# Two edits in the second feed-forward layer: an earlier place for four seven-product units, and another order of the row tiles in every down-projection

## The chip, the cores and the metric

The kernel runs as one launch on one core of a Trainium2 chip. The metric is the device time of that launch in microseconds (us); lower is better. Times of the kernel before are the median of three runs.

## What is computed

Two layers of an encoder trunk on 256 tokens of width 2048, in float32. The first layer mixes tokens by pooling and grouped-query attention, the second by a bidirectional matrix-memory recurrence. Each mixer is followed by the same feed-forward block, and only that block is touched here. Cut to what matters:

```python
D_MODEL, SEQ, D_FF = 2048, 256, 5632

def conv_ffn(x, w_up, conv_w, conv_b, w_down):
    u = x @ w_up                                   # 256 x 11264: a gate half and a value half
    up = jnp.pad(u, ((0, 0), (1, 1), (0, 0)))
    u = c[0] * up[:, :-2] + c[1] * up[:, 1:-1] + c[2] * up[:, 2:] + conv_b
    gate, val = jnp.split(u, 2, axis=-1)
    return (jax.nn.silu(gate) * val) @ w_down

for layer in range(2):
    h = rms_norm(x, norm_mix[layer])
    x = x + mixer(h)                               # attention + pooling, then the recurrence
    x = x + conv_ffn(rms_norm(x, norm_ffn[layer]), w_up[layer], conv_w[layer], conv_b[layer], w_down[layer])
```

## The kernel before

**Number format.** Every float32 operand of a matmul is split into a high and a low part (`hl`, `xx`, `g` hold both). A product is three matmuls: high by high, high by low, low by high. Weights come from memory in entries of 128 x 1024 floats (512 KB). For each entry SyncE (SP) issues the load into a tile `w`, ScalarE (ACT) rounds it to the high part (line 152), and VectorE (DVE) subtracts to get the low part (line 153). The class `Stream` does this in the order of one list for the whole program; in a feed-forward layer it loads up to eight entries ahead of the one TensorE (PE) uses and splits up to four ahead.

**The hidden layer in chunks.** The 5632 hidden columns are 44 row tiles of 128, in six chunks of 4, 8, 8, 8, 8 and 8 (`FCH`). The tiles of a chunk are kept in one buffer `g` (`gt` in the code), rows 0 to 7; two such buffers alternate between the chunks. A chunk is made by the up-projection and then read by the down-projection of that chunk, in four column blocks of 512 (`down`, one accumulation in PSUM for each block).

**Two ways to make row tiles.** A plain row tile (`up`) takes four weight entries of 16 matmuls each, and is followed by a tail: ScalarE copies the sum, VectorE adds and scales it (lines 446 and 990), then the convolution (lines 971, 972, 974), the gate (977, 978) and the split into high and low (979 on ScalarE, 980 on VectorE). Four row tiles together can instead be made by a *unit* (`quads`), which computes a 2 x 2 block product with seven block products in place of eight. A unit takes 28 entries with 6 matmuls each: eight that are accumulated in two PSUM banks, eight in two further banks, and twelve that add to them. The weight sums that it needs are made beforehand in device memory by accumulating transfers issued from GpSimd (POOL); the steps of that work (`_make_steps`) are tied to fixed positions in the list of entries. For eight of the last twelve entries of a unit VectorE adds two halves of the entry first (line 140).

When a unit's last product is done, two tasks are queued: `finish` of its third and fourth row tile 3 us later, and `finish` of its first and second row tile 11 us later (lines 1085 and 1086). Each task makes one row tile, waits 4 us, and makes the other: four transposes on PE (line 1096), a copy on ScalarE (line 1098), then the tail. These delays are in a virtual time that is advanced as matmuls are issued. PE runs strictly in the written order; on ScalarE, VectorE and SP a planner orders the instructions by times that it works out itself.

For the second half of a chunk (rows 4 to 7), the rows thus get ready in the order 6, 7, 4, 5.

**Order of the work.** `_ffn_plan(layer)` writes the order of PE's work in a feed-forward layer. It lists slots: one slot is one entry of a plain row tile (`n`, 16 matmuls) or one entry of a down-projection (`d`, two row tiles, 12 matmuls). `UNITS[layer]` then gives for each unit its chunk, its half, a first and a last slot, and how its sums are made; the 28 entries of the unit (`s`) are spread between these two slots. The second layer has six units: the first half of chunk 3, and the second half of chunks 1, 2, 3, 4 and 5. From slot 72 on, its slots are: 72 to 87 the down-projection of chunk 2; 88 to 103 the plain rows of chunk 4; 104 to 119 the down-projection of chunk 3; 120 to 135 the plain rows of chunk 5; 136 to 151 the down-projection of chunk 4; then the down-projection of chunk 5, whose last column block is written apart (`down_end`).

```python
    for c, h, lo, hi, kind in UNITS[layer]:
        one, two = 2 * m, m + m // 2                    # m = 8: 16 and 12 entries
        long = 1.25 if kind == 3 else 1.0
        step = (hi - lo - 3) / (one * long + two)
        for k in range(one + two):
            at = k * long if k < one else one * long + k - one
            here[int(lo + at * step + (3 if k >= one else 0))].append(("s", c, h))
```

Two things guard the units. The second half of a unit's first sixteen entries waits until both `finish` tasks of the unit before it have been issued (`late`, line 1046). And the transposes of `finish` use the same two PSUM banks that this second half uses.

In `down`, `kts` is the order in which the row tiles of `gt` are read, two for each weight entry; `_ffn_order` puts the entries of the weights in the same order.

Of the kernel before, what the change touches and what calls it, by code (L numbers as in the profile page):

```python
# [30 lines left out]
DFF = 5632  # L31
FT = DFF // P
FCH = [4, 8, 8, 8, 8, 8]
CH = 8
NEG = -1.0e30
NGATE = 96 + 8
# [28 lines left out]
class Stream:  # L65
# [16 lines left out]
    def load(self, pieces=1):  # L82
        i = self.n_load
        src = self.srcs[i]
        kind, src = src if isinstance(src, tuple) else ("plain", src)
        w = self.home(i, True).tile([P, CH * P], F32, tag="w", name=f"w{i}")
        if kind in ("made", "have"):
            width = n = CH * P
            at = 0
# [56 lines left out]
    def split(self, then=None):  # L146
        i = self.n_split
        self.sums(i)
        w, n, width = self.w.pop(i)[:3]
        hl = self.home(i, False).tile([P, 2, CH * P], F32R, tag="hl", name=f"hl{i}")  # L150
        for c in range(0, width, n):
# [82 lines left out]
def trunk(ctx: ExitStack, tc: tile.TileContext, gx, xT, xn, call, catt, cml, weights, make, out):  # L234
# [169 lines left out]
    def mov_part(ps, act, kts, first, last):  # L404

        n = len(kts)
        hl = None
        for i, k in enumerate(kts):
            if i % 2 == 0:
                hl = st.next()  # L410
            src, c = act(k), i % 2 * 512
            wh, wl = hl[:, 0, c : c + 512], hl[:, 1, c : c + 512]
            for t in range(2):
                xh, xl = (src[:, j, t * P : t * P + P] for j in range(2))
                mm(ps[:, t], xh, wh, first and i == 0, False)
                mm(ps[:, t], xh, wl, False, False)
                mm(ps[:, t], xl, wh, False, last and i == n - 1)
            wv.tick(1.29)

    def mov_group(act, name, width=512, before=None, after=None):  # L420

        ps = mmp.tile([P, 2, 512 if width > 256 else width], F32, tag="mm", name=name)
        per = CH * P // width
        hl = None
# [27 lines left out]
    def residual(ps, b, eng=None):  # L452
        for t in range(2):
            xs = x[:, t, b * 512 : b * 512 + 512]
            v.tensor_add(xs, xs, ps[:, t])
# [495 lines left out]
    def ffn_layer(layer, norm, nxt):  # L951
        with ExitStack() as es:
# [29 lines left out]
            def up(f, gt, i):  # L982
                ps = mmp.tile([P, 2, 2, S], F32, tag="mm", name=f"up{layer}_{f}")
                for q in range(KT // 4):
                    stat_part(ps, xx, list(range(4 * q, 4 * q + 4)), q == 0, q == KT // 4 - 1)
                    if q < KT // 4 - 1:
                        yield
                wv.until(lambda: norm.R is not None)
                u = gather(tp, ps, f"up{layer}_{f}")
                v.tensor_mul(u, u, bc(norm.R, 2))  # L990
                tail(u, f, gt, i)
# [111 lines left out]
            def down_end(gt, b, kts):  # L1103

                parts = [(0, 0, 512), (1, 0, 512)]
                pss = [psp.tile([P, 512], F32, tag="ps", name=f"end{i}") for i in range(2)]
                n = len(kts)

                def terms(i, k, hl):
                    t, c0, c1 = parts[i]  # L1110
                    ps = pss[i][:, : c1 - c0]
                    wh, wl = (hl[:, j, k % 2 * 512 + c0 : k % 2 * 512 + c1] for j in range(2))
                    xh, xl = (gt[:, k, j, t * P : t * P + P] for j in range(2))
                    mm(ps, xh, wh, k == kts[0], False)
                    mm(ps, xh, wl, False, False)
                    mm(ps, xl, wh, False, k == kts[-1])

                for k in kts[:-2]:
                    if k % 2 == 0:
                        hl = st.next()  # L1120
                    for i in range(2):
                        terms(i, k, hl)
                hl = st.next()
                for i, (t, c0, c1) in enumerate(parts):
                    for k in kts[-2:]:
                        terms(i, k, hl)
                    xs = x[:, t, b * 512 + c0 : b * 512 + c1]
                    v.tensor_add(xs, xs, pss[i][:, : c1 - c0])
                    nc.sync.dma_start(out[:, t, b * 512 + c0 : b * 512 + c1], xs)

            def down(c, gt, b):
                kts = list(range(FCH[c]))
                last = c == len(FCH) - 1
                if last and nxt is None and b == NB - 1:
                    down_end(gt, b, kts)
                    return
                ps = mmp.tile([P, 2, 512], F32, tag="mm", name=f"dn{layer}_{c}_{b}")
                for k in range(0, len(kts), 2):
                    mov_part(ps, lambda k: gt[:, k], kts[k : k + 2], k == 0, k == len(kts) - 2)
                    if k < len(kts) - 2:  # L1140
                        yield
                residual(ps, b)
                if last and nxt is None:
                    nc.sync.dma_start(out[:, :, b * 512 : b * 512 + 512], x[:, :, b * 512 : b * 512 + 512])
                elif last:
                    nxt.add(b)
                yield
# [15 lines left out]
            def g_of(c):  # L1163
                if c not in gts:
                    gts[c] = actp.tile([P, 8, 2, S], F32R, tag=f"B{c % 2}", name=f"g{layer}_{c}")
                return gts[c]

            for step in _ffn_plan(layer):
                kind, c = step[:2]
                key = step[:3]  # L1170
                if key not in run:
                    f0 = sum(FCH[:c])
                    run[key] = (up(f0 + step[2], g_of(c), step[2]) if kind == "n" else
                                down(c, gts[c], step[2]) if kind == "d" else
                                quads([f0 + 4 * step[2] + j for j in range(4)], c, 4 * step[2], f"{layer}_{c}{step[2]}",
                                      (c, step[2]) in apart))
                next(run[key], None)
# [15 lines left out]
def _stat(w, kts):  # L1193

    k = len(kts)
    t = w.reshape(k, P, 2, P)[:, :, :, :]
    return t.reshape(k // 4, 4, P, 2, P).transpose(0, 2, 1, 3, 4).reshape(k // 4, P, CH * P)


def _mov(w):  # L1200

    return w.reshape(-1, 2, P, 512).transpose(0, 2, 1, 3).reshape(-1, P, CH * P)

# [38 lines left out]
def _down_chunks(w):  # L1242
    out, k0 = [], 0
    for n in FCH:
        rows = w[k0 * P : (k0 + n) * P]
# [4 lines left out]

UNITS = (
    ((1, 1, 17, 38, 2), (2, 1, 45, 64, 2), (3, 1, 71, 100, 3), (4, 1, 107, 129, 2), (5, 1, 136, 158, 2)),
    ((1, 1, 17, 37, 2), (2, 1, 38.5, 59, 2), (3, 0, 60.5, 80, 2), (3, 1, 81.5, 99, 2), (4, 1, 100.5, 123, 2),
     (5, 1, 124.5, 146, 2)),
)


def _ffn_plan(layer):

    slots = []  # L1260
    for c, n in enumerate(FCH):
        fill = [("n", c, i) for i in range(n) if not any(u[0] == c and u[1] == i // 4 for u in UNITS[layer])]
# [7 lines left out]
        for e in fill:  # L1270
            slots += [e] * (4 if e[0] == "n" else FCH[e[1]] // 2)
    here = [[] for _ in slots]
# [29 lines left out]
def _ffn_order(layer, up, dn, four, last):  # L1302

    pos, seq = {}, []
    m = KT // 2
    d0 = [sum(FCH[:c]) // 2 * NB for c in range(len(FCH))]
    for step in _ffn_plan(layer):
        kind, c, i = step
        n = pos.get(step, 0)
        pos[step] = n + 1  # L1310
        if kind == "n":
            seq.append(up[(sum(FCH[:c]) + i) * 4 + n])
        elif kind == "d":
            seq.append(dn[d0[c] + i * (FCH[c] // 2) + n])
        else:
            u = [e[:2] for e in UNITS[layer]].index((c, i))
            made = UNITS[layer][u][4]
            if n >= 2 * m and (n - 2 * m) % 3 == 2:
                seq.append(last[u, (n - 2 * m) // 3])
                continue  # L1320
            second = n >= m if made in (1, 2) else n % 2
            at = (n - 2 * m) // 3 * 2 + (n - 2 * m) % 3 if n >= 2 * m else n % m if made in (1, 2) else n // 2
            q, key = four[u, at], f"{layer}{c}{i}_{at}"
            if n >= 2 * m:
                seq.append(("made", ((key, 1, 2), q[:, 1024:1536])) if made == 1 else ("left", q[:, 512:1536]))
            elif second:
                seq.append(("made", ((key, 2, 4),)) if made in (1, 2) else ("chain", q[:, 1024:2048]))
            else:
                seq.append((("made", "have")[made == 3], (q[:, 0:512], (key, 0, 1))) if made else ("sum", q[:, 0:1024]))
    return seq  # L1330
# [124 lines left out]
```

## Time and profile before

| | us |
|---|---|
| median of 3 runs | 2166.53 |
| lowest and highest run | 2166.33, 2166.71 |
| the profiled execution, device time | 2165.74 |
| its span, first to last instruction | 2164.0 |
| PE busy, share of the span | 2152.8 (99%) |
| PE weight loads (PEld) | 1822.8 (84%) |
| VectorE (DVE) busy | 1734.3 (80%) |
| ScalarE (ACT) busy | 1321.4 (61%) |
| GpSimd (POOL) busy | 301.6 (14%) |

The profile is one execution. Its span lies 1.7 us below that execution's own device time, and that lies 0.8 us below the median. A busy engine in the profile is one that executes; an instruction that waits for another engine shows as idle time in front of it, with the instruction that ended the wait behind an arrow. The ends of matmuls are modelled, so that a matmul looks longer than the distance to the next one; distances between starts are the pace. The column of the granted clock says what share of its full speed PE was given.

### The profile page before, as it was taken

The numbers are of one execution on the slowest core, as the hardware profiler recorded it, in microseconds if no ns is written. First come the engines' busy times: TensorE is split into PE (matmuls) and PEld (weight loads), VectorE is DVE, ScalarE is ACT, GpSimd is POOL, SyncE is SP. The second block draws the span as 40 slices with busy tenths as digits, with TensorE's granted clock in tenths as the row PEclk, the third lists the DMA queues.
The fourth block names the chain that finished last, engine by engine and source line by source line (L and its number), as shares of the span: only waits on it lengthen the run. The fifth ranks groups of instructions, "written<-read, shape, count | busy, mean of one in ns | idle before, by whom it ended". The sixth has DMA issues, their size and how long they took to land.

```text
span 2164.0 us, 31051 instructions
## 1 busy us (share of the span) xinstructions
PE 2152.8 (99%) x10824; PEld 1822.8 (84%) x10824; DVE 1734.3 (80%) x2417; ACT 1321.4 (61%) x1856; POOL 301.6 (14%) x376
## 2 busy tenths in 40 slices
PE   9999999999999999999999999999999999999998
PEld 7888888888888888889888888888888888878887
DVE  7686698989889888867767676669898978888985
ACT  7665566766557565755555454556676756665763
POOL 0222111111111111111111111110111111100000
PEclk9999999999999999999999999999999999999999
DMA  9989899999999999979898888978999999988772
GB/s 352 253 230 254 256 254 351 307 344 313 307 339 321 338 324 342 315 206 270 236 267 250 255 246 247 268 228 253 330 328 339 322 327 344 307 283 260 256 257 92
DMA packets 213727, 615.03 MB, mean 284 GB/s; under 512 B 27354, under 2 KB 29698, under 8 KB 213570
## 3 DMA queue, kind: packets, MB, share of 16 engines
q1 hardware_dynamic: 173216, 544.01, 71.5%
q0 software_dynamic: 37280, 65.30, 19.7%
q10 hardware_dynamic: 3074, 3.75, 0.6%
q8 instruction: 84, 1.38, 0.2%
q14 instruction: 73, 0.60, 0.1%
HBM read 610.81 MB, written 132.16 MB: 343 GB/s over the span
## 4 chain that ended last, share of the span: by engine, by line
PE 99%; DVE 1%; issue 0%; ACT 0%; DVEq 0%; ACTq 0%
PE up L281 23%; PE dn L281 21%; PE p L281 19%; PE op L281 8%; PE mv L281 4%; PE mq L281 4%; PE mk L281 4%; PE mo L281 4%; PE qproj L281 3%; PE kproj L281 1%; PE pool L281 1%; PE vproj L281 1%; PE tr L1096 1%; PE av L281 1%; PE qk L281 1%; PE end L281 1%
## 5 line engine op out<-in xcount | busy, mean ns | idle before, releaser
L153 DVE TENSOR_TENSOR hl<-w,hl 128x1024 fp32r<-128x1024 f32 (+1 forms) x904 | 1089.3, 1217 | 307.7 <-ACT hl L152 290.5
L152 ACT CAST hl<-w 128x1024 fp32r<-128x1024 f32 (+2 forms) x903 | 936.2, 1048 | 634.6 <-PE dn L281 106.2
L281 PE MATMUL up<-xx,hl 128*128 128x512 f32 (+1 forms) x2816 | 514.4, 337 | 0.0
L281 PEld LDWEIGHTS up<-xx,hl 128*128 128x128 f32 x2816 | 446.9, 188 | 70.7
L281 PE MATMUL dn<-hl,g 128*128 128x512 f32 x2064 | 495.7, 392 | 6.3 <-ACT g L979 6.3
L281 PEld LDWEIGHTS dn<-hl,g 128*128 128x128 f32 x2064 | 386.4, 189 | 87.9 <-ACT g L979 7.9
L281 PE MATMUL p<-hl,sx 128*128 128x512 f32 x1056 | 280.8, 391 | 0.0
L124 POOL DMA_DIRECT2D G<-in_q x176 | 147.6, 840 | 802.3 <-DMA G<-in_q 795.4
L281 PEld LDWEIGHTS p<-hl,sx 128*128 128x128 f32 x1056 | 194.1, 188 | 37.2
L128 POOL DMA_DIRECT2D G<-G x160 | 140.4, 881 | 602.4 <-DMA G<-in_q 285.1
L281 PE MATMUL p<-hl,xx 128*128 128x512 f32 x792 | 217.0, 391 | 0.0
L281 PEld LDWEIGHTS p<-hl,xx 128*128 128x128 f32 x792 | 145.0, 188 | 27.3
L281 PE MATMUL mk<-xx,hl 128*128 128x512 f32 (+1 forms) x512 | 92.2, 338 | 0.0
L281 PE MATMUL mq<-xx,hl 128*128 128x512 f32 (+1 forms) x512 | 92.2, 337 | 0.0
L281 PE MATMUL mv<-hl,xx 128*128 128x512 f32 (+2 forms) x480 | 91.8, 350 | 0.0
L281 PE MATMUL op<-hl,cat 128*128 128x512 f32 x384 | 91.6, 393 | 0.0
L281 PE MATMUL mo<-hl,xx 128*128 128x512 f32 x384 | 90.5, 391 | 0.0
L281 PE MATMUL op<-hl,mcat 128*128 128x512 f32 x384 | 89.5, 392 | 0.0
L281 PEld LDWEIGHTS mq<-xx,hl 128*128 128x128 f32 x512 | 79.3, 188 | 11.6
L281 PEld LDWEIGHTS mk<-xx,hl 128*128 128x128 f32 x512 | 79.1, 188 | 11.4
L281 PEld LDWEIGHTS mv<-hl,xx 128*128 128x128 f32 x480 | 78.3, 189 | 11.2
L281 PEld LDWEIGHTS op<-hl,mcat 128*128 128x128 f32 x384 | 71.5, 188 | 14.6
(242 smaller groups left out, 1873.5 us busy)
## 6 DMA issues: line engine op xcount, KB each, us to landing
w<-in_up SPq DMA_DIRECT2D x176, 512.0 KB, 6.8
w<-in_dn SPq DMA_DIRECT2D x176, 512.0 KB, 6.7
w<-in_m_in SPq DMA_DIRECT2D x124, 512.0 KB, 5.9
w<-in_q SPq DMA_DIRECT2D x96, 512.0 KB, 7.9
G<-in_q SPq DMA_DIRECT2D x160, 256.0 KB, 6.5
G<-G POOLq DMA_DIRECT2D x160, 256.0 KB, 7.5
w<-G SPq DMA_DIRECT2D x80, 512.0 KB, 8.5
w<-in_a_in SPq DMA_DIRECT2D x46, 512.0 KB, 7.2
```

Source lines behind the costliest of these rows:

```text
L124: pin(add.dma_start(G[r, 0:512], src[r, 512:1024], accum_op=ALU.add))
L128: pin(add.dma_start(G[:, at : at + 512], G[:, of : of + 512], accum_op=ALU.add))
L152: (self.nc.vector.tensor_copy if i + c == 0 else self.nc.scalar.copy)(hl[:, 0, c : c + n], w[:, c : c + n])
L153: self.nc.vector.tensor_sub(hl[:, 1, c : c + n], w[:, c : c + n], hl[:, 0, c : c + n].bitcast(F32))
L281: pe.matmul(out_, lhsT, rhs, start=start, stop=stop, skip_group_check=True)
L1096: pe.transpose(tr[:, j, t * P : t * P + P], src[:, c : c + P], ident)
```

## The change

The third to sixth unit of the second layer get other first and last slots: (60.5, 80) becomes (60, 79), (81.5, 99) becomes (80, 97), (100.5, 123) becomes (98.5, 121) and (124.5, 146) becomes (122.5, 144). The first two units stay. By the lines quoted above, the first and the last of a unit's 28 entries fall behind these slots:

| unit | its rows | before | after |
|---|---|---|---|
| third | chunk 3, rows 0 to 3 | 60 to 79 | 60 to 78 |
| fourth | chunk 3, rows 4 to 7 | 81 to 98 | 80 to 96 |
| fifth | chunk 4, rows 4 to 7 | 100 to 121 | 98 to 120 |
| sixth | chunk 5, rows 4 to 7 | 124 to 145 | 122 to 143 |

The steps that make the weight sums keep their positions in the list of entries.

In every down-projection of eight row tiles, of both layers, the row tiles are read in the order 0, 1, 2, 3, 6, 7, 4, 5 instead of 0 to 7, and the weight entries are listed in that order. For the first chunk, of four row tiles, nothing changes.

```diff
+DORDER = (0, 1, 3, 2)
...
             def down(c, gt, b):
-                kts = list(range(FCH[c]))
+                kts = [2 * k + j for k in DORDER[: FCH[c] // 2] for j in range(2)]
...
 UNITS = (
...
-    ((1, 1, 17, 37, 2), (2, 1, 38.5, 59, 2), (3, 0, 60.5, 80, 2), (3, 1, 81.5, 99, 2), (4, 1, 100.5, 123, 2),
-     (5, 1, 124.5, 146, 2)),
+    ((1, 1, 17, 37, 2), (2, 1, 38.5, 59, 2), (3, 0, 60, 79, 2), (3, 1, 80, 97, 2), (4, 1, 98.5, 121, 2),
+     (5, 1, 122.5, 144, 2)),
 )
...
         elif kind == "d":
-            seq.append(dn[d0[c] + i * (FCH[c] // 2) + n])
+            seq.append(dn[d0[c] + i * (FCH[c] // 2) + DORDER[n]])
```

## The prediction, made before the changed kernel was seen

> **What bounds the kernel now.** First the page's table of engines: which engine is nearly full, and how much it lacks.
>
> ```profile
> span 2164.0 us, 31051 instructions
> PE 2152.8 (99%) x10824; PEld 1822.8 (84%) x10824; DVE 1734.3 (80%) x2417; ACT 1321.4 (61%) x1856; POOL 301.6 (14%) x376
> ```
>
> PE is the bound; 11.2 us of the span are without a matmul. Next, PE's waits: what ended them.
>
> ```profile
> PE dn L281 <- ACT g L979: 6.3, 3, 3.7
> PE wps L305 <- DVE pad L674: 1.2, 1, 1.2
> ```
>
> Three waits of a down-projection (`dn`) for a row tile's high part (`g`, line 979) make 6.3 us; PE waits for nothing else but at the start. Now where they are, and what PE did behind them: instructions in order of time, with the idle time in brackets, then the chain that ended last.
>
> ```profile
> 1909.21 0.84 PE L281 MATMUL p<-hl,sx 128*128 128x512 f32 x3
> 1913.34 0.40 ACT L979 CAST g<-y 128x256 fp32r<-128x256 f32 x1
> 1913.79 3.16 PE L281 MATMUL dn<-hl,g 128*128 128x512 f32 x6 [3.73 <-ACT g L979]
> 1917.27 0.39 ACT L979 CAST g<-y 128x256 fp32r<-128x256 f32 x1
> 1917.71 2.93 PE L281 MATMUL dn<-hl,g 128*128 128x512 f32 x6 [0.76 <-ACT g L979]
> ...
> 2115.71 5.74 PE L281 MATMUL dn<-hl,g 128*128 128x512 f32 x24
> 2122.81 0.40 ACT L979 CAST g<-y 128x256 fp32r<-128x256 f32 x1 [1.31 <-DVE y L978]
> 2123.26 3.04 PE L281 MATMUL dn<-hl,g 128*128 128x512 f32 x12 [1.82 <-ACT g L979]
> ```
>
> ```profile
> 1889.94 0.68 PE p L281 x3
> 1920.64 4.15 PE p L281 x12
> 1924.79 2.72 PE dn L281 x12
> 2123.26 26.16 PE dn L281 x114
> ```
>
> The first place is the third slot of chunk 3's down-projection (slot 106): rows 4 and 5, the unit's first two, come last and are waited for one after the other. The second is row 5 of chunk 5, 40 us before the end. The chain also shows that 12 matmuls behind the first place took 4.15 us, where 12 others took 2.72. The granted clock (the column before the DMA share) says why:
>
> ```profile
> 1909.89:1913.79 3.90, 0.17 (x1) 0.00 (x1) 3.90 (x6) 3.85 (x7) 0.79 (x1) 0.93 1.05 361
> 1913.79:1917.71 3.92, 3.16 (x6) 1.67 (x7) 3.81 (x11) 2.11 (x5) 0.00 (x0) 0.50 1.04 379
> 1917.71:1920.64 2.93, 2.93 (x7) 2.26 (x8) 1.16 (x3) 0.41 (x1) 0.82 (x1) 0.50 0.48 158
> 1920.64:1924.79 4.15, 4.15 (x13) 3.27 (x13) 1.70 (x2) 2.09 (x2) 0.84 (x1) 0.65 0.56 91
> 2120.00:2125.00 5.00, 3.18 (x14) 2.22 (x13) 2.68 (x5) 1.81 (x4) 0.00 (x0) 1.00 0.62 208
> ```
>
> After 3.73 us of idle time PE got half its clock for 6.85 us; after 1.82 us it kept all of it.
>
> **What the two places cost.** A slot of 12 matmuls takes 2.72 us, one matmul 0.227. First place: the three matmuls that start at 1909.21 hold PE for 0.68 (the chain's x3 row), to 1909.89. From there to 1924.79 PE issues 24 matmuls (6, 6 and 12), worth 5.44 us, in 14.90: 9.46 us lost, of which 4.5 are waits in the table and the rest is clock and the low parts. Second place: 1.82 of wait, and 114 matmuls in 26.16 where 25.84 are due, 0.32: 2.1 us lost. Together 11.6.
>
> **Moving the units and the row order, at the first place.** Here the account is VectorE's.
>
> ```profile
> 1877.98 0.69 ACT L1083 ACTIVATE c<-p,re_n 128x512 f32<-128x512 f32 x1 [0.32 <-PE p L281]
> ...
> 1877.90:1917.70 39.80, 35.31 (x175) 28.75 (x173) 38.12 (x60) 30.75 (x49) 5.56 (x7) 0.94 1.04 349
> ...
> 1870.61 3.50 DVE L153 TENSOR_TENSOR hl<-w,hl 128x1024 fp32r<-128x1024 f32 x3 [0.83 <-ACT hl L152]
> 1836.54 8.35 PE up L281 x48
> 1927.51 1.36 PE p L281 x6
> 2100.43 0.44 PE tr L1096 x4
> ```
>
> Line 1083 reads the unit's last sum, so its last product ended at 1877.94. VectorE (third busy time of the window's row) then worked 38.12 of 39.80 us until row 5 was there: it is full, and splits of weights stand between the steps of the tail. PE's prices: a plain slot 2.78 (8.35 for 48), a unit's entry 1.36, a down slot 2.72, a set of transposes 0.44. Before, row 4 is reached after 5 plain slots (99 to 103), 2 down slots, 8 entries of the next unit and 4 sets of transposes: 13.9 + 5.4 + 10.9 + 1.8 = 32.0, and the trace has 1909.89 - 1877.94 = 31.95. Row 5, six matmuls later, is wanted at 33.3; its high part was there at 1917.66, 39.7 after: 6.4 late.
>
> After the change the unit ends behind slot 96 and row 4 is read in slot 107, the fourth: 7 plain slots (97 to 103), 3 down slots, 13 entries, 4 sets: 19.5 + 8.2 + 17.7 + 1.8 = 47.1 us, and row 5 at 48.4. That is 15.1 more, 2.72 of it from the row order alone. In them PE uses 23 entries where it was 15: VectorE has 8 more splits, at 3.50/3 = 1.17 each 9.4. Of 15.1 us 5.7 are left, against 6.4 late: I take 0.7 us of wait at this place.
>
> That residue is the unknown of the sum. Low end: the last plain row tile of chunk 4 had already taken VectorE time before row 5 (its lines 446 and 990 at 1910.13 and 1911.86), and may now come behind it: then there is no wait, and a wait can't be negative. High end: the tail of chunk 4's second plain row tile was done when the unit ended; it now starts 8 us before that end instead of 18 and can fall into the stretch.
>
> ```profile
> 1910.13 0.69 DVE L446 TENSOR_TENSOR tb_up<-up,tb_up 128x512 f32<-128x512 f32 x1
> 1911.86 0.69 DVE L990 TENSOR_TENSOR tb_up<-tb_up,R 128x512 f32<-128x512 f32 x1
> 1913.60 0.88 DVE L972 SCALAR_TENSOR_TENSOR y<-tb,cst,y 128x255 f32<-128x255 f32 x2
> 1914.39 0.42 DVE L980 TENSOR_TENSOR g<-y,g 128x256 fp32r<-128x256 f32 x1
> 1914.73 0.88 DVE L974 SCALAR_TENSOR_TENSOR y<-tb,cst,y 128x255 f32<-128x255 f32 x2
> 1916.77 0.42 DVE L978 TENSOR_TENSOR y<-y 128x256 f32<-128x256 f32 x1
> ```
>
> A whole tail is the sum of these six, 4.0 us, so the high end is 4.7. I stay at 0.7, since the row of the stretch itself gives it.
>
> A wait between 1.82 and 3.73 us has no row; the clock fell after the longer and not after the shorter. In a sentence apart: the Trainium skill (TensorE: Matmul & The Clock Gate, Part 1: The HAM clock gate) puts the fall behind a whole idle window of about 3.4 us, by which a residue of 3 us would cost 3 and give 2157.9, while by the nearest row here (3.73) it would cost the 9.46 and give 2164.4; both rows agree with the page, and neither tests the edge.
>
> **At the second place.** Before, row 5 is read 6 down slots, 5 rows and 4 sets of transposes after the unit's last product: 16.3 + 6.8 + 1.8 = 24.9. Now the unit ends behind slot 143: 8 down slots and 7 rows (0 to 3, 6, 7, 4) make 21.8 + 9.5 + 1.8 = 33.1. 8.2 more, less 3 more splits (3.5), leaves 4.7 against 2.1: this wait goes.
>
> **What is moved beside that, at no cost.** The row order in other chunks and in the first layer: as many matmuls and bytes; PE waits for no row tile there, and rows 6 and 7, now read 2.72 us sooner, are made 8 us before rows 4 and 5. Without that cover it would cost up to 2.72 a chunk. Next, the sums in device memory: a unit's entries pass SP's queue up to two entries sooner, but by the places in `kernel` the step that makes the sixth unit's last sum stands 44 entries ahead of that sum's first use, then still 42, some 75 us or more; GpSimd's queue isn't touched. The `late` guard: between the last entry of the fifth unit and the second half of the sixth lie 7 slots and 8 entries, 29 us of virtual time, against the 19 (11 + 4 + 4) that `finish` needs. PSUM: that second half wants the banks of the transposes; the fourth copy of the fifth unit was there 19.9 us after its end (1993.0 to 2012.9), against 32 us now.
>
> ```profile
> 1993.03 0.69 ACT L1083 ACTIVATE c<-p,re_n 128x512 f32<-128x512 f32 x1 [0.32 <-PE p L281]
> 2012.27 0.57 ACT L1098 COPY tb<-tr 128x512 f32<-128x512 f32 x1
> ```
>
> Uncovered, PE would stand before that second half until the copy, 1 or 2 us.
>
> **The sum.** 2164.0 - 9.46 - 2.1 + 0.7 = 2153.1 us of span. The profiled execution took 1.7 more than its span and was 0.8 below the median: 2155.6, 0.5% faster. About 0.2% (4.3 us) is what a measurement of this kernel can tell from no change.
>
> **Rivals.** *The wait stays.* VectorE sets when row 5 is ready. At the high end of 4.7 us the wait is longer than the 3.73 that halved the clock, and the first place costs its 9.46 as before: only 2.1 is gained, 2164.4, no difference to tell. For it: VectorE full in that stretch. Against: it needs a whole foreign tail on top of the count.
>
> *The weights come late.* By slot 104 the new order has used two entries (1.05 MB) more, and the transfers are at 1.04 share and 349 GB/s there: 3.0 us, 2158.6. Against: from 1650 to 1910, splits waited for loads 1.7 and 0.8 us in all.
>
> ```profile
> ACT hl L152 <- DMA w<-in_q: 1.7, 1, 1.7
> ACT hl L152 <- DMA w<-G: 0.8, 1, 0.8
> ...
> 1895.00:1900.00 5.00, 5.00 (x30) 4.27 (x29) 4.95 (x8) 3.48 (x6) 0.82 (x1) 1.00 1.03 395
> ```
>
> The Trainium skill (DMA: Bandwidth & Descriptors, Where 436 GB/s comes from) speaks for this rival: it puts a core's share of device memory at about 358 GB/s, which would leave nothing above the 349 and give 2.9 us; the 395 GB/s of the window above does not bear that out.
>
> *Slower: the splits fall behind.* Slots 91 to 103 now hold 13 plain slots and 20 unit entries, 63.3 us of PE. VectorE has 33 splits (38.6), 8 half sums at line 140 (0.69 each, 5.5), 4 sums at the unit's end (2.9), 4 rows of the unit (2.6 each, 10.4), and 4 plain tails (15.9): 73.3, 10.0 over. The decision falls where this exceeds the four entries split ahead, 4 x 1.92 = 7.7 us: then PE waits for `hl`. A wait of the first place's kind here and one behind the fifth unit cost 9.46 each: 2174.5.
>
> ```profile
> 1868.77 0.69 DVE L140 TENSOR_TENSOR w<-w 128x512 f32<-128x512 f32 x1
> 1881.96 0.74 DVE L1074 SCALAR_TENSOR_TENSOR c<-p,re_n,c 128x512 f32<-128x512 f32 x1
> ```
>
> Against: durations overlap, so the count is high; the last tail (4.0) can wait for 30 us; and the same count for slots 92 to 105 before (66.0 us of PE, 74.5 of VectorE) is 8.5 over, where no split was waited for.
>
> **How the numbers follow.** Forecast 0.74, the wait that stays 0.10, late weights 0.09, splits behind 0.07. Faster by over 0.2%: 0.74 + 0.09 = 0.83; within: 0.10; slower: 0.07. The range begins at 2153.8 (no residue, 2154.9, and 1.1 for how far one profiled execution can stand from the median, here 0.8) and ends at 2161.5, above late weights and most of a residue together (2158.6 + 2.9); the rest, 0.17, lies outside.
>
> **What would show it.** Right: no wait for `g` above 1 us, clock 1.00 at all of chunk 3's down-projection, span near 2153. Wrong: a wait at the fourth slot of that projection with VectorE full before it; or PE waiting for `hl` between 1830 and 1900.

## The result, and the profile after

The changed kernel takes 2156.86 us (median of 4 runs, 2156.79 to 2156.92) against 2166.62 before (median of 4 runs, one more than in the table above): a ratio of 0.9953, 95% interval 0.994 to 0.9966, or 9.8 us. The forecast was 2155.6 within 2153.8 to 2161.5. The first lines of the page after, and PE's and its weight loads' waits, each with total, number and longest in us (line numbers are one higher than before):

```profile
span 2155.0 us, 31044 instructions
PE 2148.3 (100%) x10824; PEld 1821.3 (85%) x10824; DVE 1733.2 (80%) x2417; ACT 1322.3 (61%) x1856; POOL 301.7 (14%) x376
```

```profile
PE tr L1097 <- DVE c L1074: 1.7, 1, 1.7
PE wps L306 <- DVE pad L675: 1.2, 1, 1.2
PE p L282 <- DVE hl L154: 0.2, 1, 0.2
...
PEld tr L1097 <- DVE c L1074: 1.9, 1, 1.9
PEld p L282 <- DVE hl L154: 0.5, 1, 0.5
```

All three waits for a row tile are gone. In their place stand two smaller ones of VectorE's making: a transpose of the fourth unit waits for line 1074, and a product of the same unit for a split. The chain shows the down-projections of chunk 3 and of the end at full pace (2.72 us for 12 matmuls; 162 in 36.77):

```profile
1907.11 2.72 PE dn L282 x12
1909.83 2.72 PE p L282 x12
1912.55 2.72 PE dn L282 x12
1915.27 1.36 PE p L282 x6
1916.62 2.72 PE dn L282 x12
1919.35 2.72 PE p L282 x12
1922.07 2.72 PE dn L282 x12
...
2103.71 36.77 PE dn L282 x162
```

Instructions around the fourth unit's end, in order of time:

```profile
1870.18 1.42 PE L282 MATMUL p<-hl,sx 128*128 128x512 f32 x5 [0.22 <-DVE hl L154]
1873.02 0.69 ACT L1084 ACTIVATE c<-p,re_n 128x512 f32<-128x512 f32 x1 [0.22 <-PE p L282]
1876.29 0.27 PE L1097 MATMUL tr<-cst,c 128*128 128x128 f32 x1
1877.48 0.69 DVE L1074 TENSOR_TENSOR c<-c,c 128x512 f32<-128x512 f32 x1
1878.22 0.55 PE L1097 MATMUL tr<-cst,c 128*128 128x128 f32 x3 [1.66 <-DVE c L1074]
...
1913.06 0.41 ACT L980 CAST g<-y 128x256 fp32r<-128x256 f32 x1
1914.34 0.42 DVE L981 TENSOR_TENSOR g<-y,g 128x256 fp32r<-128x256 f32 x1
```

The last two rows make row 5 of chunk 3 (the order of the program's instructions says which cast is which row). Its high part is there at 1913.47, 40.5 us after the unit's last product (1872.98), and it is read at 1922.07 + 1.36 = 1923.43.

**The balance.** Of the 11.6 us that the two places cost, all came back. About 2.4 (1.9 and 0.5) are the new waits: 9.2, and the spans differ by 9.0.

### The profile page after: what moved, and what is told of

It reads as the page before. It is cut to its first block, busy times and chain, and to the rows that moved or that the text cites. A ratio compares the mean times of both kernels' runs of the same rounds, so it can differ in the third digit from the quotient of the medians.

```text
span 2155.0 us, 31044 instructions
## 1 busy us (share of the span) xinstructions
PE 2148.3 (100%) x10824; PEld 1821.3 (85%) x10824; DVE 1733.2 (80%) x2417; ACT 1322.3 (61%) x1856; POOL 301.7 (14%) x376
## 4 chain that ended last, share of the span: by engine, by line
PE 98%; DVE 1%; issue 0%; ACT 0%; DVEq 0%; ACTq 0%
PE up L282 22%; PE dn L282 22%; PE p L282 19%; PE op L282 8%; PE mv L282 4%; PE mq L282 4%; PE mk L282 4%; PE mo L282 4%; PE qproj L282 3%; PE pool L282 1%; PE kproj L282 1%; PE vproj L282 1%; PE tr L1097 1%; DVE hl L154 1%; PE av L282 1%; PE qk L282 1%
## 5 line engine op out<-in xcount | busy, mean ns | idle before, releaser
L282 PEld LDWEIGHTS mq<-xx,hl 128*128 128x128 f32 x512 | 79.3, 188 | 11.6
```

The lines of the kernel that those rows point to most:

```text
L282: pe.matmul(out_, lhsT, rhs, start=start, stop=stop, skip_group_check=True)
```

## The experiments

Each time is compared with runs of the kernel before on the same chip. Three chips were used. The kernel before took 2166.36 beside the row order alone, the units alone, the later transposes and the one wait filled; 2166.77 beside all three waits filled; and 2166.24 beside the other three kernels.

**The row order alone.** The old `UNITS`, the new `DORDER`.

> The changed kernel with the old slots of all units: only the row order 0, 1, 2, 3, 6, 7, 4, 5 is new. Theory A (a wait costs its own length, and as much again or more when it is long enough for the clock to halve): row 4 is wanted 2.72 us later, at 1912.6 by the trace of before, and is there at 1913.7; row 5 is there at 1917.7. Two waits of about 1.1 and 2.5 us, no fall of the clock, 3.7 us lost in place of 9.5; the wait 40 us before the end goes (2.1). 2166.6 - 5.7 - 2.1 = 2158.8. Theory B (the loss goes with the length of the waits, whatever the clock does): 3.7 of the 6.5 us of waiting stay, so 5.5 of 9.5, and 2160.5. Theory C (the rows come when VectorE gets to them, and it drifts as PE does): the rows slip by the 2.72 us too, the first place stays, 2164.5.

Measured: 2162.18, ratio 0.998 (0.9971 to 0.9989), between theory B and theory C. Row 4 came when it had come before (1913.80) and its wait went, but row 5 came later than before, as C says. The profile of this kernel, instructions in order of time, then a window behind the wait (busy times, then granted clock, DMA share and GB/s):

```profile
1914.80 1.22 DVE L154 TENSOR_TENSOR hl<-w,hl 128x1024 fp32r<-128x1024 f32 x1
1916.73 2.35 DVE L154 TENSOR_TENSOR hl<-w,hl 128x1024 fp32r<-128x1024 f32 x2
1920.24 0.41 ACT L980 CAST g<-y 128x256 fp32r<-128x256 f32 x1 [2.29 <-DVE y L979]
1920.70 2.68 PE L282 MATMUL dn<-hl,g 128*128 128x512 f32 x6 [3.79 <-ACT g L980]
```

```profile
1920.70:1923.18 2.48, 2.48 (x7) 1.71 (x7) 1.39 (x4) 0.82 (x2) 0.00 (x0) 0.66 0.95 248
```

Three more splits than before stand on VectorE among row 5's steps: 3.5 us at 1.17. That the planner put them there because PE, now 2.72 us farther, frees their buffers sooner is argued, not shown. The row is there at 1920.65 instead of 1917.66, and one wait of 3.79 us again takes part of the clock. At the second place 0.6 us of wait stays, for the low part of the row. The order alone is worth 4.2 us of the 9.8.

**The units alone.** The new `UNITS` with `DORDER = (0, 1, 2, 3)`.

> The changed kernel with the old row order 0 to 7: only the slots of four units are new. In the trace of after row 5 of chunk 3 is there at 1914.8 at the latest and read at 1923.4, so 8.7 us early. Theory A: with the old order it is read 2.72 us sooner, still 6 us late enough, so no wait for a row tile at chunk 3, and the same time as after, 2156.9. Near the end, rows 4 and 5 of chunk 5 were there 2109.2 and 2110.8 to 2111.2, and are read in the trace of after from 2112 on, with the old order from 2109.2: about 0 to 1 us of wait there. 2156.9 to 2157.9. Theory B (the residue of my forecast, rows just in time): a wait of 0.7 + 2.7 = 3.4 us at chunk 3, 2160.3 or more.

Measured: 2156.78, ratio 0.9956 (0.9943 to 0.9968): theory A, without its end wait. The expectation had read the place of that wait some 4 us too early: by the chain of this kernel rows 4 and 5 of chunk 5 are read from 2113.5 on, and their parts were all there at 2111.5. There is no wait for a row tile anywhere, and the same wait at the transposes as after (1.6). With the units sooner, the row order adds nothing that can be measured: 2156.78 against 2156.86.

**Later transposes.** The changed kernel with

```diff
-                            wv.add(finish(c12, c22, fs[2:], gt, i0 + 2, name), 3.0)
+                            wv.add(finish(c12, c22, fs[2:], gt, i0 + 2, name), 5.0 if name == "1_31" else 3.0)
```

> The changed kernel, but the first finish task of the fourth unit (chunk 3, rows 6 and 7) is queued 5 us behind the unit's end in place of 3. In the trace of after, PE stands 1.7 us (1.9 for its weight loads) in the second of these transposes, until VectorE has made the sum at line 1074. Theory A: that wait is the larger part of what after lost against the sum forecast; with 2 us of other matmuls put in front it goes, 2156.9 - 1.8 = 2155.1. Theory B: VectorE is so full there that the wait turns up at the next instruction that needs it (splits or the third transposes), 2156.9.

Measured: 2154.87, ratio 0.9947 (0.9933 to 0.9961): theory A. The wait is gone and did not turn up elsewhere; PE's waits in this kernel:

```profile
PE wps L306 <- DVE pad L675: 1.2, 1, 1.2
PE p L282 <- DVE hl L154: 0.2, 1, 0.2
```

**One wait filled.** The kernel before with

```diff
                 for k in range(0, len(kts), 2):
+                    if (layer, c, b, k) == (1, 3, 0, 4):
+                        for i in range(34):
+                            t = i % 2
+                            mm(ps[:, t, 0:S], gt[:, 3, 1, t * P : t * P + P], gt[:, 2, 1, :], False, False)
```

> The kernel before, with 34 more matmuls of 128 x 256 (0.11 us each, about 3.9 us) in front of row 4 in the first column block of chunk 3's down-projection, where PE stood idle 3.7 us. They multiply the low part of row 3 by that of row 2, and add a term to the sum that the reference does not have. Theory A (the idle time halves the clock): PE is as late for row 4, but keeps its clock; of 9.5 us lost about 6.5 stay, 2166.6 - 3.0 = 2163.6, with the granted clock 1.00 behind it. Theory B (the slow matmuls behind the wait come from something else, such as rows or weights that arrive slowly): 2166.6, and the matmuls from 1914 to 1925 are as slow as before.

Measured: 2165.11, ratio 0.9996 (0.9987 to 1.0005): not settled by the time. Its 11 runs lie in three groups, near 2163.8, 2165.0 and 2166.3, with a mean granted clock of 1.000, 0.999 and 0.998; the fastest group lies where theory A put the time. The windows of its profiled execution, one of the slowest group, show why:

```profile
1909.93:1914.01 4.08, 4.08 (x36) 4.07 (x35) 4.08 (x6) 3.85 (x7) 0.79 (x1) 1.00 1.05 341
1914.01:1916.10 2.09, 1.81 (x8) 0.86 (x6) 2.09 (x7) 1.21 (x3) 0.00 (x0) 1.00 1.03 386
1916.10:1917.75 1.65, 0.00 (x0) 0.00 (x1) 1.55 (x5) 0.90 (x3) 0.00 (x0) 0.98 1.09 372
1917.75:1920.48 2.73, 2.73 (x7) 2.05 (x7) 1.16 (x3) 0.41 (x1) 0.82 (x1) 0.50 0.73 206
...
2120.00:2125.00 5.00, 3.18 (x9) 2.23 (x8) 1.99 (x3) 0.94 (x4) 0.00 (x0) 0.75 0.59 201
```

Behind the filled place the clock is 1.00. But row 5 is still waited for, 1.66 us, and there it halves; and at the second place the wait of 1.8 us, which had kept its clock in the profile of before, now lowers it to 0.75.

**All three waits filled.** The kernel before with the same matmuls in front of each wait:

```diff
+                def act(k):
+                    for i in range({(1, 3, 0, 4): 34, (1, 3, 0, 5): 22, (1, 5, 0, 5): 16}.get((layer, c, b, k), 0)):
+                        t = i % 2
+                        mm(ps[:, t, 0:S], gt[:, 3, 1, t * P : t * P + P], gt[:, 2, 1, :], False, False)
+                    return gt[:, k]
...
-                    mov_part(ps, lambda k: gt[:, k], kts[k : k + 2], k == 0, k == len(kts) - 2)
+                    mov_part(ps, act, kts[k : k + 2], k == 0, k == len(kts) - 2)
```

> The kernel before, with added matmuls of 128 x 256 in front of all three waits for a row tile: 34 before row 4 and 22 before row 5 in chunk 3's first column block, 16 before row 5 in chunk 5's. As in the run that filled one wait, they add a term to the sum that the reference does not have. In that run the clock fell again behind the waits of 1.66 and 1.8 us that were left, in some executions and not in others. Theory A (every wait of 1.7 us or more can halve the clock, by when it falls): PE is as late for the rows, 6.5 + 1.8 us, but keeps its clock everywhere; 2166.4 - 3.3 = 2163.1, granted clock 1.00 behind all three, and the runs lie within 0.5 us of one another, as those of the changed kernel do. Theory B (the spread of the runs and the slow matmuls are not the clock's): 2165.1 and a spread of over 2 us, as with one wait filled.

Measured: 2163.83, ratio 0.9989 (0.998 to 0.9998): theory A. The 11 runs lie within 0.54 us, where the 15 runs of the kernel before on the same chip spread over 3.2. The clock behind the waits:

```profile
1915.00:1920.00 5.00, 4.74 (x31) 4.38 (x32) 4.16 (x11) 2.52 (x6) 0.00 (x0) 1.00 0.91 321
1920.00:1925.00 5.00, 5.00 (x24) 4.14 (x23) 3.13 (x3) 3.17 (x3) 0.82 (x1) 1.00 0.63 107
2115.00:2120.00 5.00, 5.00 (x25) 4.15 (x24) 4.31 (x8) 3.41 (x5) 0.00 (x0) 1.00 0.52 164
2120.00:2125.00 5.00, 5.00 (x29) 4.23 (x29) 2.15 (x4) 1.46 (x2) 0.00 (x0) 1.00 0.53 184
```

Filling idle time with 72 useless matmuls made the kernel 2.9 us faster. So about 3 of the 11.6 us that the two places cost were clock, and the rest waiting. The trace of before gives the same for the first place: from the start of row 5's matmuls at 1917.71 to 1924.79 PE took 7.08 us for 18 matmuls, which are due in 4.08.

**Less work for VectorE.** The kernel before with

```diff
                 for j in range(2):
...
+                    if layer == 1 and f in (26, 27, 30):
+                        continue
                     v.scalar_tensor_tensor(y[:, j, 1:S], u[:, j, 0 : S - 1], cw(tl, 0), y[:, j, 1:S],
```

> The kernel before, with the two side taps of the convolution (lines 972 and 974, four instructions of 0.40 us each row) left out for three row tiles of the second layer: rows 6 and 7 of the fourth unit and the third plain row of chunk 4. Rows 4 and 5, which PE waits for, keep their whole tail. Theory A (VectorE is full there, and rows 4 and 5 come when its work is done): 4.8 us less in front of them, row 4 in time, row 5 about 1.6 late; of the 9.5 us at the first place 1.6 to 4 stay: 2166.4 - 5.5 to 7.9 = 2158.5 to 2160.9. Theory B (the rows are late by the fixed distance of the transposes and the chain of steps of one row): 2166.4. Theory C (the planner puts later splits into the freed time, as in the run with the row order alone): between, 2163.

Measured: 2164.4, ratio 0.999 (0.9981 to 0.9999): nearest to theory C by its time, but not by its mechanism. Row 4 is in time; row 5 comes 2.2 us sooner (1915.43 against 1917.66), not 4.8, and is waited for alone. An instruction of this kernel (its line numbers are two higher than those of before behind the added lines), and a window some us before it, with VectorE still full (third busy time):

```profile
1915.47 2.87 PE L281 MATMUL dn<-hl,g 128*128 128x512 f32 x6 [3.96 <-ACT g L981]
```

```profile
1905.00:1910.00 5.00, 5.00 (x24) 4.13 (x23) 5.00 (x8) 4.22 (x7) 0.00 (x0) 1.00 1.05 327
```

From the unit's end to row 5, VectorE was busy 4.3 us less than before (33.76 against 38.07). It made as many splits, 20 in both with one cut by the window's start, so the freed time was not filled with later splits, as theory C has it. Instead VectorE stood idle 2.0 us longer (3.64 against 1.65), and 1.7 us of its idle time was one wait of a split for a load.

That VectorE's load bears on when rows 4 and 5 come is shown, since they moved with it while their own tails stayed whole; theory B falls. But it is not VectorE alone. In the kernel before, row 4's last step on VectorE ahead of its high part ended at 1910.22, 0.33 us after PE wanted the row; the cast then stood on ScalarE behind other work until 1913.34. Some instructions of the kernel before:

```profile
1909.80 0.42 DVE L978 TENSOR_TENSOR y<-y 128x256 f32<-128x256 f32 x1
1910.84 1.04 ACT L152 CAST hl<-w 128x1024 fp32r<-128x1024 f32 x1
1911.77 0.69 ACT L1064 ACTIVATE c<-p,re_n 128x512 f32<-128x512 f32 x1
1912.35 1.09 ACT L971 ACTIVATE y<-tb,cst 128x256 f32<-128x256 f32 x2
1913.34 0.40 ACT L979 CAST g<-y 128x256 fp32r<-128x256 f32 x1
```

So 3.1 of the 3.73 us that PE waited for row 4 lay in the order of ScalarE's work. No run changed that order alone.

**The third and fourth unit alone.** The changed kernel with the fifth at (100.5, 123) and the sixth at (124.5, 146).

> The changed kernel, but the fifth and the sixth unit keep their old slots: only the third and the fourth unit come sooner, with the new row order. Theory A: the first place is gone (with the 1.9 us that the transposes wait), at the second place the row order alone leaves about 0.6 us, as in the run with the row order alone: 2156.9 + 0.6 = 2157.5. Theory B: the second place slips as the first did in that run and costs its 2.1: 2159.0. Theory C: with the fifth unit's first entries two slots farther from the end of the fourth, VectorE has room and the transposes don't wait: 2155.6.

Measured: 2158.18, ratio 0.9963 (0.995 to 0.9975), between A and B. The transposes wait as after. At the second place the low part of row 5 is waited for:

```profile
PE dn L282 <- DVE g L981: 0.6, 1, 0.6
```

With the weight loads' wait for it (1.0) the second place still costs 1.4 us, by the spans 2156.4 and 2155.0. So moving the fifth and sixth unit is worth about 1.4, and the rest of what the units bring lies at the third and the fourth, which this run doesn't part; the waits that went were for rows of the fourth.

**A looser fourth unit.** The kernel with the later transposes and

```diff
-    ((1, 1, 17, 37, 2), (2, 1, 38.5, 59, 2), (3, 0, 60, 79, 2), (3, 1, 80, 97, 2), (4, 1, 98.5, 121, 2),
+    ((1, 1, 17, 37, 2), (2, 1, 38.5, 59, 2), (3, 0, 60, 79, 2), (3, 1, 80, 98, 2), (4, 1, 99.5, 121.5, 2),
```

> The kernel with the later transposes (2154.9), and the fourth unit over one slot more, 80 to 98 in place of 80 to 97, the fifth at 99.5 to 121.5. In the trace with the later transposes PE still waits 0.2 us (0.5 for its weight loads) for a split in the fourth unit's dense end. Theory A: that wait goes and row 5 of chunk 3 has 8.7 - 4 us to spare: 2154.4. Theory B: the rows slip with the unit and the planner, and a wait for row 5 comes back: 2156 or more.

Measured: 2154.66, ratio 0.9946 (0.9934 to 0.9959), span 2152.5. In the second layer PE waits for nothing any more; its waits in this kernel:

```profile
PE wps L306 <- DVE pad L675: 1.2, 1, 1.2
PE kproj L282 <- ACT xx L345: 0.3, 1, 0.3
```

The spans say that half a microsecond went (2153.0 to 2152.5); the medians, 2154.87 and 2154.66 on two chips, don't tell these two apart. Both beat the changed kernel by some 2 us. 2164.0 - 11.6 would be 2152.4, so the size given to the two places was right.

## Why the prediction was right, point by point

**The two places and their price.** Right, and shown: with every wait of the second layer gone, the span is 2152.5 against the 2152.4 that 11.6 us allow. That part of the first place's 9.46 is clock was read from the windows, and the filled waits show it. The second place's price holds for the profiled execution; in others its wait costs clock too (0.75 and 0.66 in the profiles of one wait filled and of less work for VectorE). The prediction put the late rows to VectorE alone; for row 4 most of the wait was ScalarE's order, as shown under less work for VectorE. The change removes the wait either way, since it moves the moment when PE wants the row.

**The residue at chunk 3.** The sum had 0.7 us of wait for row 5. There is none, and row 5's high part is 10.0 us early (1913.47 against 1923.43). The step that failed is "VectorE has 8 more splits" *before* row 5, 9.4 us. Measured from the unit's end, row 5 took 39.7 us before and 40.5 after: 0.8 in place of 9.4. Between the unit's end and row 5's high part VectorE made 20 splits before and 19 after, counted with one cut by the window's start or end: none of the 8 stood in front of row 5. The second place says the same. There the sum charged 3 more splits, and row 5 of chunk 5 came 26.8 us behind the copy of its unit's last sum before (2096.39 to 2123.21) and 25.1 after (2084.14 to 2109.24). To charge the whole demand of a stretch to one instruction in it holds only if the rest stands ahead of that instruction. The row-order run shows the other case: there three added splits did get in front (23 in the same stretch), and the row came 3.0 us later. An error of 10.7 us in when row 5 comes (0.7 late forecast, 10.0 early measured) cost the forecast only 0.7 us, because it fell on the side where no wait is left; that was luck.

**The wait that was not in the sum.** The 0.7 was put at the wrong place, and 2.4 us of wait arose elsewhere; the two errors have opposite signs, which helped the forecast to within 1.3 us. The moved unit ends in a denser stretch, and there VectorE is at its limit; the third busy time in a window of after:

```profile
1870.00:1880.00 10.00, 8.15 (x43) 6.86 (x44) 10.00 (x15) 6.95 (x11) 1.64 (x2) 1.00 1.05 378
```

What came late was not a row but the sum at line 1074, wanted by the transposes 3 us after the unit's end, and one split. The products that this sum needs last are those of the unit's last entry but one. Before, the unit's last two entries fell behind slots 97 and 98, with a plain slot between them; now both fall behind slot 96, since the entries of the unit are 0.50 slots apart in place of 0.52. Instructions of the kernel before (line 1073 is 1074 after), then of after:

```profile
1870.90 2.89 PE L281 MATMUL p<-hl,sx 128*128 128x512 f32 x12
1873.63 2.94 PE L281 MATMUL up<-xx,hl 128*128 128x512 f32 x16
1876.41 1.53 PE L281 MATMUL p<-hl,xx 128*128 128x512 f32 x6
1877.95 0.69 DVE L1073 TENSOR_TENSOR c<-c,c 128x512 f32<-128x512 f32 x1
1881.26 0.60 PE L1096 MATMUL tr<-cst,c 128*128 128x128 f32 x4
```

```profile
1871.45 1.53 PE L282 MATMUL p<-hl,xx 128*128 128x512 f32 x6
1872.82 3.64 PE L282 MATMUL up<-xx,hl 128*128 128x512 f32 x20
```

From the end of those products to the transposes PE took 7.6 us before (1873.63 to 1881.26) and 4.8 after (1871.45 to 1876.29). VectorE had the sum ready 5.0 us behind them before (1878.64) and 6.7 after (1878.17). So the lost plain slot took 2.8 us of room. The other 1.7 us lie in VectorE's queue, where four steps of the tail of chunk 4's second plain row now stand among the sums. Two us of later transposes were enough to end the wait, and the looser unit, which keeps them, also has the plain slot back. The prediction looked at the transposes' PSUM banks and put VectorE's four sums only into the count of the slower rival; it did not ask what waits for them. This is that rival's mechanism at its mildest: its count of 10.0 us over in slots 91 to 103 gave 0.5 us of wait for splits, not waits of the first place's kind. PE waiting for `hl` between 1830 and 1900 was one of the signs named for being wrong; it came, but too small to undo the gain.

**The rivals.** The wait for row 5 did not stay. Late weights are not seen: PE's only wait for a split was on VectorE's subtraction, with transfers at 378 GB/s, and from 1650 to 1930 ScalarE's casts of weights waited 0.8 us in all for loads. The edge of about 3.4 us that the prediction cites from the Trainium skill (TensorE: Matmul & The Clock Gate, Part 1: The HAM clock gate) is not borne out: in one run waits of 1.66 and 1.8 us brought the granted clock to 0.50 and 0.75, and in another one of 1.82 us left it at 1.00.

**The free terms.** The row order elsewhere, the sums in device memory and the guards cost nothing: no wait in the profile of after points at them. A copy of a unit's sum that stands at 1688.16 before stands at 1688.25 after, so the row order up to there cost no more than 0.1 us.

## What to carry to other kernels

When one engine sets the time and another is full, a place in the order is worth what the full engine's queue makes of it: ask which of its instructions stand ahead of the awaited one, and don't charge it with work that is wanted later. After moving a dense stretch, look at every result that the main engine takes from the full one at the new place, small sums before transposes as well as the large tails. A delay of two virtual microseconds for one task was worth 2 us here; the new row order was worth 4 by itself and nothing beside the moved units.

## What the runs showed of the hardware that was not expected

A short wait of PE can cost its clock or not. In the profiled executions 1.82 us left it at 1.00 (before), and so did 1.66 us at the transposes (after); but 1.66 and 1.8 us brought it to 0.50 and 0.75 (one wait filled), and another 1.82 us to 0.66 over the next 5 us (less work for VectorE). The executions can spread with such waits in the program: 2.2 us in 21 runs of before, 2.7 with one wait filled. With none of a microsecond left but the one at the start they lie within 0.54 (all three waits filled). The four runs of after, with its one wait of 1.66 us, lie within 0.13 at a mean clock of 1.000. What in the timing decides it was not tried.
